# Two PSUM banks for products of weights and one for the transposes and rows behind them, in place of a shared set of three

## The chip, the cores and the metric

The kernel runs on one core of one Trainium2 chip. The metric is the device time of one execution in microseconds (us); lower is better. Time before is a median of three executions, and one further execution was profiled.

## The reference

One layer of a hybrid decoder, 2048 tokens behind 16 meta tokens, width 1024, everything in float32. The normalised input is projected by one wide matrix; the parts feed three causal mixers of four heads of 128 each (stick-breaking attention, a gated delta rule called GDN here, and HGRN2, called HG); each mixer's output is gated, projected by its own branch matrix, weighted by a sigmoid mix and summed; the sum is projected once more and added to the input.

```
xn = rms_norm(h, norm_w)
proj = einsum('btd,dn->btn', xn, w_in)          # 12*512 + 8 + 3*1024 columns
o_sb = stick_breaking_attention(rms_norm(q), rms_norm(k), v) * silu(sb_z)
o_gd = rms_norm(gated_delta_rule_chunked(l2_norm(gq), l2_norm(gk), gv, beta, g)) * silu(gd_z)
o_hg = rms_norm(hgrn2_chunked(silu(hg_q), hk, hg_i, log(forget))) * silu(hg_z)
gates = sigmoid(mix)                            # (b, t, 3, 1024)
y = sum over the three branches of gates[b] * einsum('btw,wd->btd', o_b, w_branch[b])
out = h + einsum('btd,de->bte', y, w_out)
```

## The kernel before, in words

The tokens are worked in four groups of 512 (`j` = 0 to 3; group 0 carries the 16 meta tokens too and computes them in two halves of 272 and 256 columns). Everything is held transposed: width on the 128 partitions, tokens in the free dimension. Every float32 product is three matmuls (`mm3`, lines 167 to 169): the operands are split in a high and a low part, and high by high, high by low and low by high are summed in one PSUM bank. A projection by 128 columns of a weight matrix is therefore 24 matmuls of 128x512 (8 pieces of the width, three each) into one bank.

The dense stream (`dense_work`) yields after each piece: per group, attention's projections (`sb_proj`, four heads), GDN's rows and projections (`gdn_rows`, `gdn_proj`, `gdn_gates`), HG's (`hg_proj`), the branch products (`branch`) and the output (`outp`). The three scans, attention (`z`, `tr` and `av` tiles, lines 521 to 565), GDN (855 to 1023) and HG (1151), are chains of small steps over TensorE (PE), ACT, DVE and POOL; `weave` advances the dense stream between their steps in proportion to estimated times, so that PE has products of weights to run while a chain is on another engine. The emitted program is reordered afterwards by the framework's scheduler, so a change of buffers changes the order on every engine. A product that stands between two steps of a scan is called a filler here.

The eight PSUM banks: four for `z` and `tr` (scan tiles), one for `av` (attention's output), three called `acc`. All of `acc` comes from one rotating function, `p_acc`, whether the tile is a projection of 24 matmuls or the four small transposes behind it. Such followers are: the column sums of squares (`sum_cols`, transposes at L380 in `to_tokens`), the broadcast of a row of scales back over the partitions (`row_bcast`, L176 and for the meta tokens L180), the turn of the values into token order (`post_v`, L380), GDN's rows (`gdn_rows`, L700) and HG's first state (L1117). Each is read by ACT, DVE or both (for example L454, which multiplies the keys by the row) and its bank is free again when the last reader is done. They are put off by `later` to the end of the next projection, so they come out between two projections. While the GDN and HG scans run (`n_acc[1]` true) every fourth tile of `p_acc` goes to the `av` bank, which attention doesn't use then.

Line numbers are those of the kernel before; in the kernel after the same lines stand 9 or 10 lower (L167 is L176, L176 is L185, L380 is L389, L558 is L567), and tile numbers are 3 higher.

Of the kernel before, what the change touches and what calls it, by code (L numbers as in the profile page):

```python
# [7 lines left out]
F32 = mybir.dt.float32  # L8
# [4 lines left out]
PSUM = bass.MemoryType.PSUM  # L13
DRAM = bass.MemoryType.DRAM

P = 128
# [23 lines left out]
def kernel(  # L40
# [21 lines left out]
    nc = tc.nc  # L62
# [3 lines left out]
    wpool = ctx.enter_context(tc.tile_pool(name="wpool", bufs=3))  # L66
    pool = ctx.enter_context(tc.tile_pool(name="pool", bufs=2))
    dram = ctx.enter_context(tc.tile_pool(name="dram", bufs=1, space=DRAM))
    ps_acc = ctx.enter_context(tc.tile_pool(name="ps_acc", bufs=3, space=PSUM))
    ps_z = ctx.enter_context(tc.tile_pool(name="ps_z", bufs=4, space=PSUM))  # L70
    ps_av = ctx.enter_context(tc.tile_pool(name="ps_av", bufs=1, space=PSUM))

# [2 lines left out]
    def nm(s):  # L75
        uid[0] += 1
        return f"{s}_{uid[0]}"
# [6 lines left out]
        return pool.tile(list(shape), dt, tag=tag, name=nm(tag), bufs=bufs or BUFS[tag])  # L84


    n_acc = [0, False]

    def p_acc():
        n_acc[0] += 1  # L90
        if n_acc[1] and n_acc[0] % 4 == 0:
            return ps_av.tile([P, 512], F32, tag="av", name=nm("av"))
        return ps_acc.tile([P, 512], F32, tag="acc", name=nm("acc"))

    def p_z():
        return ps_z.tile([P, 512], F32, tag="z", name=nm("z"))
# [74 lines left out]

    def row_bcast(r, cols, mcol):

        pt = p_acc()
        for n, c in enumerate(cols):
            nc.tensor.transpose(pt[:, n * P : (n + 1) * P], r[:, c : c + 1].broadcast_to([P, P]), ident)  # L176
        res = [(slice(META, WQ), pt)]
        if mcol is not None:
            pm = p_acc()
            nc.tensor.transpose(  # L180
                pm[:, :META], r[:META, mcol : mcol + 1].broadcast_to([META, P]), ident[:META, :META]
            )
            res.append((slice(0, META), pm[:, :META]))
        return res
# [10 lines left out]
    def norm_x0():  # L195

        xt, sq, raws = [], [], []
        for k in range(KC):
            t = slot("D")
# [7 lines left out]
        for k in range(KC):  # L207
            t = slot("D")
# [10 lines left out]
        ps = p_acc()  # L219
# [13 lines left out]
        xl = [xpool.tile([P, WQ], F32R, tag=f"xl{k}", name=nm("xl")) for k in range(KC)]  # L233
        rows = []
        for i, (a, b) in enumerate(HALVES):
            rb = p_acc()
            c = 0
            if i == 0:
                nc.tensor.transpose(
                    rb[:, :META], r[:META, NT : NT + 1].broadcast_to([META, P]), ident[:META, :META]  # L240
                )
                c = META
            for n in (2 * i, 2 * i + 1):
                nc.tensor.transpose(rb[:, c : c + P], r[:, n : n + 1].broadcast_to([P, P]), ident)
                c += P
            rows.append(rb)
# [115 lines left out]

    def sum_cols(src, dst, c, meta_c=None, ps=None):

        ps = ps or p_acc
        pt = to_tokens(src, ps())
        nc.vector.tensor_reduce(
            dst[:, c : c + NT], pt.rearrange("p (n d) -> p n d", n=NT), mybir.AxisListType.X, ALU.add
        )
        if meta_c is not None:  # L370
            pm = ps()
            nc.tensor.transpose(pm[:META, :P], src[:, :META], ident)
            nc.vector.tensor_reduce(
                dst[:META, meta_c : meta_c + 1], pm[:META, :P], mybir.AxisListType.X, ALU.add
            )
# [33 lines left out]
    def sb_proj(j, xs, h, st):  # L409
# [64 lines left out]
        vm = slot("vmp", (96, HD), F32R, 2) if m0 else None  # L474

        def post_v():
            pt = to_tokens(vraw, p_acc())
            nc.scalar.copy(vh, pt)
            sub_lo(vl, pt, vh, nc.vector)
            if m0:  # L480
                pm = p_acc()
                nc.tensor.transpose(pm[:META, :P], vraw[:, :META], ident)
                nc.scalar.copy(vm, zero1[:96].broadcast_to([96, HD]))
                for r0 in (0, 32):
                    nc.scalar.copy(vm[r0 : r0 + META], pm[:META, :P])
                sub_lo(vm[64 : 64 + META], pm[:META, :P], vm[:META], nc.vector)
            if j < nq - 1:
                dv = [dram.tile([P, TQ], F32, name=nm("dv")) for _ in range(2)]
                for s_, d_ in ((vh, dv[0]), (vl, dv[1])):
                    nc.sync.dma_start(d_, s_.bitcast(F32))  # L490
                dm = []
                if m0:
                    dm = [dram.tile([96, HD], F32, name=nm("dm"))]
                    nc.sync.dma_start(dm[0], vm.bitcast(F32))
                d_kv[(j, h, "v")] = dv + dm
# [142 lines left out]
    def gdn_rows(j, xs, st):  # L638
# [12 lines left out]
        bcol = slot("bcol", (P, H, 5), F32, 2)  # L651

        def post():
            pt = p_acc()
            for n in range(NT):
                nc.tensor.transpose(
                    pt[:, n * nr : n * nr + nr], raw[:nr, META + n * P : META + (n + 1) * P], ident[:nr, :nr]
# [1 line left out]
            c8 = slot("c8", (P, 2, H, 5), F32, 1)  # L659
            if m0:  # L660
                nc.gpsimd.memset(c8, 0.0)
                pm = p_acc()
                nc.tensor.transpose(pm[:META, :36], raw[:36, :META], ident[:36, :36])
                for q in range(2):
                    nc.vector.tensor_copy(c8[:META, q, :, 4], pm[:META, 32 * q : 32 * q + H])
# [30 lines left out]
            later(lambda: post_rows(ab))  # L696

        def post_rows(ab):
            pr = p_acc()
            nc.tensor.transpose(pr[:, :P], ab, ident)  # L700
            row = slot("D", (P, 2, P))
            nc.scalar.copy(row[:, 0], pr[:, :P])
            sets = [(0, 16, P, rows)] + ([(64, H, META, rowsm)] if m0 else [])
            for p0, np_, w, dst in sets:
                al_ = row[p0 : p0 + np_, 0, :w]
                eg = row[p0 : p0 + np_, 1, :w]
                nc.vector.tensor_tensor_scan(
                    eg, al_, zero1[p0 : p0 + np_].broadcast_to([np_, w]), 1.0, ALU.mult, ALU.add
                )
                nc.vector.memset(al_[:, 0:1], 0.0)  # L710
                be = row[p0 + 32 : p0 + 32 + np_, 0, :w]
                for i, src in enumerate((al_, eg, be)):
                    nc.sync.dma_start(dst[i].rearrange("h (n t) -> (h n) t", t=w), src)
# [29 lines left out]
    def gdn_proj(j, xs, hs, st):  # L743
# [5 lines left out]
        def head(h):  # L749
# [37 lines left out]
            bvm = slot("bvm", (META, P), F32, 4) if m0 else None  # L787

            def post_v():
                pt = to_tokens(vv, p_acc())  # L790
                for n in range(NT):
                    nc.scalar.mul(bv[:, n], pt[:, n * P : (n + 1) * P], bs[:, n : n + 1])
                if m0:
                    pm = p_acc()
                    nc.tensor.transpose(pm[:META, :P], vv[:, :META], ident)
                    nc.scalar.mul(bvm, pm[:META, :P], bcol[:META, h, NT : NT + 1])

# [274 lines left out]
    def hg_proj(j, xs, h, st):  # L1072
# [23 lines left out]
        yield from proj(j, xs, CH_HI + h, True, lambda ps, a, b: nc.scalar.copy(vraw[:, a:b], ps))  # L1096
        vt = slot("D", (P, NT, P))
        def post_v():
            nc.scalar.copy(vt.rearrange("p a b -> p (a b)"), to_tokens(vraw, p_acc()))
            if m0:  # L1100
                pm = p_acc()
                nc.tensor.transpose(pm[:META, :P], vraw[:, :META], ident)
                vm = slot("vm", (META, P), F32, 2)
                nc.scalar.copy(vm, pm[:META, :P])
# [4 lines left out]
                    1.0, ALU.mult, ALU.add,  # L1109
                )  # L1110
                nc.vector.tensor_mul(km, km, kk[:, :META])
                pm = p_acc()
                nc.tensor.transpose(pm[:META, :P], km, ident)
                kmt = slot("kmt", (META, P), F32, 2)
                nc.scalar.copy(kmt, pm[:META, :P])
                pm = p_acc()
                nc.tensor.matmul(pm[:, :P], kmt, vm, start=True, stop=True)  # L1117
                nc.scalar.copy(Sh[h], pm[:, :P])

# [227 lines left out]
    def dense_work():  # L1347

        xs = norm_x0()
        for j in range(nq):  # L1350
            y, yh, yl = [None] * KC, [None] * KC, [None] * KC
            pool_share[0] = 5
            for h in range(H):
                yield from sb_proj(j, xs, h, sst)
                if j == 0 and h == 0:
                    load_levels()
            ahead = 5 * (j >= AHEAD)
# [247 lines left out]
```

## Time and profile before

| | |
|---|---|
| median of three executions | 2745.89 us (2745.52 to 2747.46) |
| profiled execution | 2744.01 us, span 2742.2 us |
| mean granted TensorE clock | 0.996 of full speed |
| PE busy | 2693.8 us, 98% of the span |
| DVE, ACT, POOL busy | 1433.0, 961.7 and 724.1 us |

PE's busy time is counted by the rows of its matmuls, whose modelled ends overlap the next start; time in which it stood is 48 us in all, 11.8 of them in the first wait after the start.

### The profile page before, as it was taken

How to read it: one execution, taken by the hardware profiler on the slowest of the kernel's cores; microseconds unless marked ns; L12 is line 12 of the kernel's file. 1: busy time of each engine (PE TensorE's matmuls, PEld its weight loads, DVE VectorE, ACT ScalarE, POOL GpSimd, SP SyncE). 2: the span in 40 equal slices, each digit the busy share in tenths (PEclk: the TensorE clock that was granted, in tenths of full speed). 3: DMA queues.
4: the chain of work that ended last, by engine and by line, in shares of the span. 5: the costliest groups of instructions: out<-in, count | busy, mean ns of one | idle time of the engine just before them, and what ended most of it. 6: DMA issues, size and time to landing. Idle time of an engine off the chain costs nothing.

```text
span 2742.2 us, 46669 instructions
## 1 busy us (share of the span) xinstructions
PE 2693.8 (98%) x17984; PEld 2248.8 (82%) x17984; DVE 1433.0 (52%) x2870; ACT 961.7 (35%) x2199; POOL 724.1 (26%) x989
## 2 busy tenths in 40 slices
PE   7999999999999999999999999999999999999999
PEld 6898788888888888888888888878888887787887
DVE  5467638635357634443255765553325577456522
ACT  5554244343346212212144641221224455312120
POOL 4555203333132401112022340111212233302111
PEclk9999999999999999999999999999999999999999
DMA  7667756679554654557755556355764454554556
GB/s 263 228 209 245 256 184 222 229 266 321 195 183 142 209 177 129 156 162 243 226 185 168 164 177 186 109 156 155 252 214 146 159 166 138 159 157 124 163 164 212
DMA packets 200834, 521.08 MB, mean 190 GB/s; under 512 B 42848, under 2 KB 44832, under 8 KB 200612
## 3 DMA queue, kind: packets, MB, share of 16 engines
q1 hardware_dynamic: 200324, 518.03, 58.7%
q8 instruction: 142, 2.33, 0.3%
q14 instruction: 80, 0.66, 0.1%
q10 hardware_dynamic: 288, 0.07, 0.0%
HBM read 397.57 MB, written 120.44 MB: 189 GB/s over the span
## 4 chain that ended last, share of the span: by engine, by line
PE 92%; DVE 4%; ACT 1%; DMA 1%; issue 1%; POOL 1%; SPq 0%; DVEq 0%; POOLq 0%; ACTq 0%
PE acc L167 21%; PE acc L168 21%; PE acc L169 21%; PE av L167 4%; PE av L168 4%; PE av L169 4%; PE tr L558 2%; PE acc L380 2%; PE z L167 1%; PE z L1151 1%; PE z L169 1%; PE z L168 1%; PE z L855 1%; PE tr L380 1%; PE tr L1236 1%
## 5 line engine op out<-in xcount | busy, mean ns | idle before, releaser
L167 PE MATMUL acc<-xh,w 128*128 128x512 f32 (+2 forms) x2248 | 858.4, 382 | 4.1 <-DVE D L454 2.2
L168 PE MATMUL acc<-xl,w 128*128 128x512 f32 (+2 forms) x2248 | 847.3, 377 | 0.3 <-DVE xl L260 0.2
L169 PE MATMUL acc<-xh,w 128*128 128x512 f32 (+2 forms) x2248 | 845.4, 376 | 1.7 <-DVE w L118 1.7
L167 PEld LDWEIGHTS acc<-xh,w 128*128 128x128 f32 x2248 | 426.4, 190 | 78.9 <-DVE D L454 3.0
L169 PEld LDWEIGHTS acc<-xh,w 128*128 128x128 f32 x2248 | 426.4, 190 | 74.6 <-DVE w L118 2.2
L168 PEld LDWEIGHTS acc<-xl,w 128*128 128x128 f32 x2248 | 426.1, 190 | 69.8 <-DVE xl L260 1.3
L530 DVE TENSOR_TENSOR_SCAN S<-S,zero 128x128 f32<-128x128 f32 (+4 forms) x216 | 199.8, 927 | 151.3 <-ACT S L524 124.0
L118 POOL TENSOR_TENSOR w<-wraw,w 128x512 fp32r<-128x512 f32 x106 | 147.9, 1396 | 274.5 <-ACT w L147 228.1
L536 POOL TENSOR_TENSOR S<-S,S 128x256 f32<-128x256 f32 (+2 forms) x108 | 96.2, 891 | 372.0 <-DVE S L530 232.2
L524 ACT ACTIVATE S<-z,rq 128x128 f32<-128x128 f32 (+4 forms) x216 | 117.0, 542 | 140.4 <-PE z L169 94.4
L147 ACT CAST w<-wraw 128x512 fp32r<-128x512 f32 x182 | 112.4, 619 | 132.9 <-PE acc L169 68.8
L736 DVE SCALAR_TENSOR_TENSOR D<-D,cw,D 128x512 f32<-128x512 f32 (+1 forms) x144 | 120.8, 839 | 21.9 <-ACT D L734 19.4
L118 DVE TENSOR_TENSOR S<-tr,S 128x512 fp32r<-128x512 f32 (+4 forms) x176 | 105.9, 607 | 44.9 <-ACT S L563 25.8
L167 PE MATMUL acc<-ob,w 128*128 128x512 f32 x312 | 124.6, 401 | 1.4 <-ACT ob L401 1.4
L168 PE MATMUL acc<-ob,w 128*128 128x512 f32 x312 | 124.5, 399 | 0.0
L169 PE MATMUL acc<-ob,w 128*128 128x512 f32 x312 | 123.7, 396 | 0.6 <-issue 0.6
L1288 POOL TENSOR_TENSOR y<-y,g 128x512 f32<-128x512 f32 x32 | 51.7, 1616 | 263.6 <-DVE g L1286 263.6
L167 PE MATMUL av<-xh,w 128*128 128x512 f32 (+2 forms) x304 | 118.5, 390 | 0.7 <-ACT D L1082 0.7
L168 PE MATMUL av<-xl,w 128*128 128x512 f32 (+2 forms) x304 | 117.7, 387 | 0.0
L169 PE MATMUL av<-xh,w 128*128 128x512 f32 (+2 forms) x304 | 117.0, 385 | 0.0
L525 ACT ACTIVATE S<-z,rq 128x128 f32<-128x128 f32 (+4 forms) x216 | 116.5, 539 | 0.0
L558 PE MATMUL tr<-ident,S 128*128 128x128 f32 (+1 forms) x608 | 102.0, 272 | 2.0 <-POOL S L536 1.7
(391 smaller groups left out, 4781.5 us busy)
## 6 DMA issues: line engine op xcount, KB each, us to landing
w<-wk SPq DMA_DIRECT2D x555, 512.0 KB, 3.6
wk<-w SPq DMA_DIRECT2D x184, 512.0 KB, 3.5
wraw<-in_w_in_dram SPq DMA_DIRECT2D x142, 256.0 KB, 4.1
D<-in_xq_dram SPq DMA_DIRECT2D x56, 256.0 KB, 4.5
S<-rows SPq DMA_DIRECT2D x48, 256.0 KB, 5.0
S<-dv SPq DMA_DIRECT2D x48, 256.0 KB, 4.6
out_dram<-D SPq DMA_DIRECT2D x32, 256.0 KB, 4.8
S<-dk SPq DMA_DIRECT2D x24, 264.0 KB, 4.1
```

The costliest lines, as they stand in the source:

```text
L118: (eng or nc.gpsimd).tensor_sub(out_, a, hi.bitcast(F32))
L147: nc.scalar.copy(hi, raw)
L167: nc.tensor.matmul(dst, lh, rh, start=first, stop=False)
L168: nc.tensor.matmul(dst, lh, rl, start=False, stop=False)
L169: nc.tensor.matmul(dst, ll, rh, start=False, stop=last)
L380: nc.tensor.transpose(pt[:, n * P : (n + 1) * P], src[:, META + n * P : META + (n + 1) * P], ident)
L524: nc.scalar.activation(pc[:, :n], z[:, :n], AF.Sigmoid, scale=rq[:, NT + i : NT + i + 1])
L525: nc.scalar.activation(at[:, :n], z[:, :n], AF.Sigmoid, scale=rq[:, i : i + 1])
L530: nc.vector.tensor_tensor_scan(pc[:, 0:n][:, ::-1], pc[:, 0:n][:, ::-1], zero1.broadcast_to([P, n]), 1.0 if carry[i] is None else pc[:, n ...
L536: eng.tensor_mul(at[:, :n], at[:, :n], pc[:, 1 : n + 1])
L558: nc.tensor.transpose(tr[:kw, i * P : (i + 1) * P], ats[i][:, a - lo : a - lo + kw], ident)
L736: nc.vector.scalar_tensor_tensor(dst[:, c0:], raw[:, c0 + i : c0 + i + n], cw[:, ci, i : i + 1], dst[:, c0:], ALU.mult, ALU.add)
```

## The change

`ps_acc` shrinks from three banks to two, and a new pool `ps_t` of one bank takes the followers: `p_t` replaces `p_acc` in `row_bcast`, `sum_cols`, the rows of the first norm, all three `post_v` and GDN's rows. Until a flag `n_acc[2]` is set, behind the first head's attention projections of group 0, `p_acc` and `p_t` together rotate through the same three banks as before. From then on products alternate between two banks, and while the GDN and HG scans run every third product, not every fourth, goes to the `av` bank. The number of banks (eight), the instructions and their counts are the same on every engine; the tiles are 378 `acc`, 181 `t` and 93 `av`, against 571 `acc` and 81 `av`.

```diff
-    ps_acc = ctx.enter_context(tc.tile_pool(name="ps_acc", bufs=3, space=PSUM))
+    ps_acc = ctx.enter_context(tc.tile_pool(name="ps_acc", bufs=2, space=PSUM))
+    ps_t = ctx.enter_context(tc.tile_pool(name="ps_t", bufs=1, space=PSUM))
...
-    n_acc = [0, False]
+    n_acc = [0, False, False]
     def p_acc():
         n_acc[0] += 1
-        if n_acc[1] and n_acc[0] % 4 == 0:
+        if not n_acc[2] and n_acc[0] % 3 == 0:
+            return ps_t.tile([P, 512], F32, tag="t", name=nm("t"))
+        if n_acc[1] and n_acc[0] % 3 == 0:
             return ps_av.tile([P, 512], F32, tag="av", name=nm("av"))
         return ps_acc.tile([P, 512], F32, tag="acc", name=nm("acc"))
+
+    def p_t():
+        if not n_acc[2]:
+            return p_acc()
+        return ps_t.tile([P, 512], F32, tag="t", name=nm("t"))
...
     def row_bcast(r, cols, mcol):
-        pt = p_acc()
+        pt = p_t()
...
     def sum_cols(src, dst, c, meta_c=None, ps=None):
-        ps = ps or p_acc
+        ps = ps or p_t
...
         def post_v():
-            pt = to_tokens(vraw, p_acc())
+            pt = to_tokens(vraw, p_t())
...
                 yield from sb_proj(j, xs, h, sst)
+                n_acc[2] = True
```

The change moves instructions. The first place is on PE in group 1's attention projections, where a row of scales for the keys (`acc_8163`, later `t_8166`) and a set of column sums (`acc_8175`) stood between two products. Before:

```order
3679 L176 MATMUL acc_8163<-ident,nr_8123 128x128 [waits Activation_49,Pool_49]
3680 L176 MATMUL acc_8163<-ident,nr_8123 128x128 x3
3681 L380 MATMUL acc_8175<-ident,D_8086 128x128 [waits DVE_49]
3682 L380 MATMUL acc_8175<-ident,D_8086 128x128 x3
3683 L167 MATMUL acc_8193<-xh_7639,w_1570_8189 128x512 [waits DMAHW6_49,DVE_49]
3684 L168 MATMUL acc_8193<-xl_7640,w_1570_8189 128x512
```

The same place on PE after, where the product is called `acc_8196`:

```order
3686 L176 MATMUL acc_8196<-xh_7738,w_1570_8192 128x512
3687 L177 MATMUL acc_8196<-xl_7739,w_1570_8192 128x512
3688 L185 MATMUL t_8166<-ident,nr_8126 128x128 [waits DVE_49,Pool_49]
3689 L185 MATMUL t_8166<-ident,nr_8126 128x128 x3
3690 L178 MATMUL acc_8196<-xh_7738,w_1570_8192 128x512
3691 L176 MATMUL acc_8196<-xh_7786,w_1570_8192 128x512
```

The row now comes after the eighth matmul of the product, in the bank of its own, and the column sums (`t_8178`) come another 16 matmuls of this product and seven of the next later.

The second place is on PE in group 0's projections for GDN (`gdn_proj`), where a head's row of scales for 512 tokens and for the 16 meta tokens (`nr_2745`) is broadcast and its values (`D_2537`) are turned. Before, all of it stands between two products:

```order
1327 L169 MATMUL acc_2802<-xh_172,w_554_2769 128x256
1328 L176 MATMUL acc_2829<-ident,nr_2745 128x128 [waits DVE_49,Pool_49]
1329 L176 MATMUL acc_2829<-ident,nr_2745 128x128 x3
1330 L180 MATMUL acc_2834<-ident,nr_2745 128x16 [waits Activation_49]
1331 L380 MATMUL acc_2838<-ident,D_2537 128x128 [waits Activation_49]
1332 L380 MATMUL acc_2838<-ident,D_2537 128x128 x3
1333 L795 MATMUL acc_2847<-ident,D_2537 16x128 [waits DVE_49]
1334 L167 MATMUL acc_2887<-xh_165,w_570_2873 128x272 [waits DVE_49]
```

On PE after, the row for the 512 tokens stands inside the next product, 18 matmuls ahead of these rows, which begin with the last matmul of that product:

```order
1371 L178 MATMUL acc_2916<-xh_175,w_573_2883 128x256
1372 L189 MATMUL t_2837<-ident,nr_2748 128x16 [waits DVE_49]
1373 L389 MATMUL t_2841<-ident,D_2540 128x128 [waits DVE_49]
1374 L389 MATMUL t_2841<-ident,D_2540 128x128 x3
1375 L864 MATMUL z_2937<-S_2868,D_2280 128x128 [waits DVE_49]
1376 L864 MATMUL z_2937<-S_2868,D_2280 128x128 x3
```

The wait for ACT ahead of the values is gone; the meta row, the values and GDN's first z tile now each wait for DVE.

The third place is on PE at the end of an attention head in group 3. `z` tiles take queries and keys, `tr` tiles turn attention weights, `av_22290` collects the output. Before:

```order
10950 L521 MATMUL z_22911<-neg_b,ident_b 128x128
10951 L558 MATMUL tr_22857<-ident,S_22848 32x128 [waits Pool_49]
10952 L558 MATMUL tr_22869<-ident,S_22848 128x128
10953 L558 MATMUL tr_22879<-ident,S_22848 128x128
10954 L167 MATMUL z_22932<-D_22420,D_22303 128x256 [waits DVE_49]
10955 L168 MATMUL z_22932<-D_22421,D_22303 128x256
10956 L169 MATMUL z_22932<-D_22420,D_22304 128x256
10957 L521 LDWEIGHTS ident_b
10958 L521 MATMUL z_22932<-neg_b,ident_b 128x128
10959 L547 MATMUL av_22290<-S_22862,vmp_22645 128x512 [waits Activation_49]
10960 L167 MATMUL av_22290<-S_22874,S_22639 128x512
```

On PE after, the turned weights are followed by products of weights, and the output's first matmul (L556, for `av_22293`) comes behind them:

```order
10938 L567 MATMUL tr_22860<-ident,S_22851 32x128 [waits Pool_49]
10939 L567 MATMUL tr_22872<-ident,S_22851 128x128
10940 L567 MATMUL tr_22882<-ident,S_22808 128x128
10941 L567 MATMUL tr_22882<-ident,S_22834 128x128
10942 L567 MATMUL tr_22882<-ident,S_22851 128x128
10943 L176 MATMUL acc_23936<-xh_20810,w_4659_23934 128x512
10944 L177 MATMUL acc_23936<-xl_20811,w_4659_23934 128x512
10945 L178 MATMUL acc_23936<-xh_20810,w_4659_23934 128x512
10946 L176 MATMUL acc_24001<-xh_20544,w_4671_23997 128x512 [waits DMAHW0_49,Activation_49]
10947 L177 MATMUL acc_24001<-xl_20545,w_4671_23997 128x512
```

Between the last `tr` row and the output's first matmul now stand 25 matmuls of two products and four transposes of a follower; before there were none. At the end of the next head (`av_22910`) it is the other way: `acc_24403` and `acc_24453`, of which 24 and nine matmuls stood inside the head's last blocks, come behind its last output matmul.

## Rows read from the trace of the kernel before

**Rows 1.** The page's part 1: busy time, share of the span, instructions.

```profile
PE 2693.8 (98%) x17984; PEld 2248.8 (82%) x17984; DVE 1433.0 (52%) x2870; ACT 961.7 (35%) x2199; POOL 724.1 (26%) x989
```

**Rows 2.** PE's waits: us in total, times, longest.

```profile
PE acc L221 <- DVE D L212: 11.8, 1, 11.8
PE z L1151 <- DVE S L1142: 4.8, 4, 2.4
PE acc L380 <- ACT D L731: 3.3, 3, 2.2
PE acc L700 <- DVE D L694: 2.6, 1, 2.6
PE acc L167 <- DVE D L454: 2.2, 4, 1.0
PE acc L239 <- POOL nr L231: 2.0, 1, 2.0
PE av L547 <- ACT S L565: 2.0, 1, 2.0
PE z L167 <- DVE S L118: 1.9, 1, 1.9
PE acc L169 <- DVE w L118: 1.7, 1, 1.7
PE tr L558 <- POOL S L536: 1.7, 1, 1.7
...
PE z L943 <- DVE S L927: 1.1, 1, 1.1
...
PE acc L380 <- ACT D L1096: 0.7, 1, 0.7
PE av L167 <- ACT D L1082: 0.7, 1, 0.7
```

**Rows 3.** Timeline around 707 us: start, length, instruction, idle before it.

```profile
707.44 0.60 PE L380 MATMUL acc<-ident,D 128*128 128x128 f32 x4
707.64 0.75 DVE L454 SCALAR_TENSOR_TENSOR D<-D,wk,acc 128x512 f32<-128x512 f32 x1 [2.96 <-PE acc L176]
...
708.44 0.51 PE L167 MATMUL acc<-xh,w 128*128 128x512 f32 x1 [0.40 <-DVE D L454]
...
709.25 0.39 PE L167 MATMUL acc<-xh,w 128*128 128x512 f32 x1
...
709.48 0.39 PE L168 MATMUL acc<-xl,w 128*128 128x512 f32 x1
```

**Rows 4.** Stretches: length, busy time per engine, then PEclk, DMA share, GB/s.

```profile
212.00:224.00 12.00, 8.87 (x52) 8.32 (x51) 8.34 (x12) 5.11 (x13) 5.91 (x5) 0.72 0.70 229
1788.00:1798.00 10.00, 7.65 (x119) 6.02 (x118) 10.00 (x25) 3.25 (x9) 1.28 (x1) 0.83 0.40 126
2270.00:2286.00 16.00, 12.10 (x59) 9.41 (x58) 11.75 (x17) 9.81 (x21) 2.37 (x10) 0.79 0.31 100
2343.00:2370.00 27.00, 22.54 (x122) 18.33 (x121) 13.47 (x22) 8.90 (x20) 6.88 (x14) 1.00 0.37 105
2496.00:2514.00 18.00, 15.89 (x463) 12.69 (x463) 18.00 (x51) 1.63 (x5) 5.27 (x2) 1.00 0.43 122
```

**Rows 5.** Timeline around 214 us, group 0's GDN projections.

```profile
211.80 2.29 POOL L125 TENSOR_TENSOR nr<-nu,mhalf 128x9 f32<-128x9 f32 x1
...
214.15 0.65 PE L176 MATMUL acc<-ident,nr 128*128 128x128 f32 x4 [0.93 <-POOL nr L125]
...
216.74 0.35 ACT L731 COPY D<-acc 128x256 f32<-128x256 f32 x1
...
217.15 1.11 PE L380 MATMUL acc<-ident,D 128*128 128x128 f32 x4 [2.20 <-ACT D L731]
```

**Rows 6.** PE's timeline at 2281 us, the output matmuls of an attention head.

```profile
2281.25 0.63 PE L168 MATMUL av<-S,S 128*128 128x512 f32 x1
2281.68 0.63 PE L169 MATMUL av<-S,S 128*128 128x512 f32 x1
```

More of the change, by code (lines that the diff above doesn't have):

```diff
@@ L178, in row_bcast @@
         if mcol is not None:
-            pm = p_acc()
+            pm = p_t()
             nc.tensor.transpose(
@@ L235, in norm_x0 @@
         for i, (a, b) in enumerate(HALVES):
-            rb = p_acc()
+            rb = p_t()
             c = 0
@@ L480, in post_v @@
             if m0:
-                pm = p_acc()
+                pm = p_t()
                 nc.tensor.transpose(pm[:META, :P], vraw[:, :META], ident)
@@ L653, in post @@
         def post():
-            pt = p_acc()
+            pt = p_t()
             for n in range(NT):
@@ L661, in post @@
                 nc.gpsimd.memset(c8, 0.0)
-                pm = p_acc()
+                pm = p_t()
                 nc.tensor.transpose(pm[:META, :36], raw[:36, :META], ident[:36, :36])
@@ L698, in post_rows @@
         def post_rows(ab):
-            pr = p_acc()
+            pr = p_t()
             nc.tensor.transpose(pr[:, :P], ab, ident)
@@ L789, in post_v @@
             def post_v():
-                pt = to_tokens(vv, p_acc())
+                pt = to_tokens(vv, p_t())
                 for n in range(NT):
@@ L793, in post_v @@
                 if m0:
-                    pm = p_acc()
+                    pm = p_t()
                     nc.tensor.transpose(pm[:META, :P], vv[:, :META], ident)
@@ L1098, in post_v @@
         def post_v():
-            nc.scalar.copy(vt.rearrange("p a b -> p (a b)"), to_tokens(vraw, p_acc()))
+            nc.scalar.copy(vt.rearrange("p a b -> p (a b)"), to_tokens(vraw, p_t()))
             if m0:
-                pm = p_acc()
+                pm = p_t()
                 nc.tensor.transpose(pm[:META, :P], vraw[:, :META], ident)
@@ L1111, in post_v @@
                 nc.vector.tensor_mul(km, km, kk[:, :META])
-                pm = p_acc()
+                pm = p_t()
                 nc.tensor.transpose(pm[:META, :P], km, ident)
@@ L1115, in post_v @@
                 nc.scalar.copy(kmt, pm[:META, :P])
-                pm = p_acc()
+                pm = p_t()
                 nc.tensor.matmul(pm[:, :P], kmt, vm, start=True, stop=True)
```

## The prediction

> **What bounds the kernel now.** I read the page first, then PE's waits over the whole span, then the busy time and granted clock of the stretches in which those waits lie, and last the timelines there. The page shows a kernel that is bound by PE: it is busy for 2693.8 us, DVE for about half the span, ACT and POOL for less [rows 1]. The reader is to see in the list of waits how little there is to win [rows 2]: PE stands for 2742.2 - 2693.8 = 48 us, and 13.8 of them belong to the first norm (L221 and L239), which the change leaves in the old rotation; what remains is at most 35 us, in many places. The stretches [rows 4] show a second cost: three of them have a mean granted clock of 0.72 to 0.83. PE was idle for 2 to 4 us in each, and part of each ran at 1.2 GHz. The output matmuls at 2281 us start 0.43 us apart [rows 6], against 0.23 at full clock [rows 3]. So a wait in these places costs more than its own length, and the change can win a wait of 2 us twice.
>
> Not all waits are for a bank. L1151 waits for DVE's chain of HG, L558 and the z product at L167 for attention's chain, L700 and L176 for rows. A new rotation reaches those only by the order of instructions.
>
> **The change part by part.** The instructions are the same, so PE's busy time stays, and each term is a wait gained or lost. A wait costs a little more than the list shows, because a matmul's row of 0.39 us overlaps the next start, 0.23 behind it [rows 3]: 0.16 us for each.
>
> *A, the joins of attention's projections.* At 707 us the row's reader, L454, takes DVE 0.75 us, the column sums on PE cover only part of it, and the next product takes over the row's bank and waits 0.40 [rows 3]. There are four such waits, 2.2 us in sum [rows 2], in groups 1, 2 and 3; with the overlap 2.2 + 4 x 0.16 = 2.8. After, the next product takes a bank of its own and the row comes eight matmuls into it; its reader has 16 + 7 matmuls (5.3 us) to be done before the bank t is wanted again. I take all: -2.8 (bounds -2.2 and -2.8).
>
> *B, two more waits for a bank.* The product that follows the values of HG in `av` (0.7) and the values behind L1096 (0.7) [rows 2]. By the order after, no turn of the `av` bank has under 3 us of PE work between, where one had 0.13; the other keeps a part. -1.2 (bounds -0.7 and -1.7).
>
> *C, group 0's GDN projections.* At 214 us POOL's power takes 2.29 us, the row waits 0.93 for it, and then the values wait 2.20 for L731, which frees a bank late because it stands in ACT's queue behind work that waits for DVE [rows 5]. PE is idle 12.00 - 8.87 = 3.1 us in this stretch, and its clock of 0.72 means 2 x 0.28 x 12 = 6.7 us at 1.2 GHz [rows 4]; the values' wait lies in these, so at least 6.7 - 2.2 = 4.5 us were worked at half rate, which loses 2.2. Another 3.3 - 2.2 = 1.1 us of waits for L731 stand elsewhere [rows 2]. Together 6.4. After, the row lies inside a product, but the meta row, the values and the first z tile follow each other with no product between, two of them in one bank. Each waits for a DVE reading; the nearest row is L454's 0.75 [rows 3], with the way there and back about 1 us each, so 2 us for the two heads in which this order appears. -4.5 (bounds -6.4, and 0 if two short waits set off the same clock).
>
> *D, GDN's scan, first step.* L943 waits 1.1 for DVE [rows 2]; it stands some 13 us of PE work later after. -1.2 with the overlap. The wait of 1.7 for a weight's low part, 3 us on, is left, as nothing there changes the load.
>
> *E, HG's scans in groups 2 and 3.* L1151's four waits, 4.8 us [rows 2]. DVE is busy 10.00 of 10 and 18.00 of 18 us there [rows 4], so the chain itself does not shorten; only products put between its steps help. In group 3 the steps now stand 1.6 to 6.4 us of PE work apart, where they came in pairs: -1.5 of the 2.1 idle. In group 2 the order is nearly the same: -0.5. Bounds 0 and -6 (all waits, and 3.4 us of half clock from 0.83 of 10 us).
>
> *F, the end of an attention head in group 3.* From 2270 to 2286 PE is idle 3.9 us, and 0.79 means 6.7 us at half clock [rows 4]. At most 1.9 of these were the second wait, so 4.8 at half rate lose 2.4: 6.3 in all. After, 25 matmuls and four transposes (25 x 0.23 + 4 x 0.11 = 6.2 us) stand between the turned weights and the output. They cover the waits of 1.7 and 1.9 [rows 2]. I leave 1.3 for the z product's half of the chain: -5.0 (bounds -6.3 and -3).
>
> *G, what F and the new order take from elsewhere.* Fillers are not made, only moved. Counting PE work between products of weights in the two orders (a z product of 272 columns as 0.13, a transpose as 0.11): the next head loses 24 + 9 matmuls from its last blocks, and a stretch of 9.0 us without a filler appears there (2.8 and 2.5 before); a further one of 8.2 us appears some 15 us before F; GDN's scan has one of 10.1 in group 0 that is new, and 14.4 in place of 10.2 in group 2. The trace of before prices such a stretch: 6.3 in F, where it is 7.9 us long. But L547's and the branch product's waits at the end of the next head already cost 4.5 us idle at full clock in 2343 to 2370 [rows 4], and stay. I take about half of F's price for the first (+3.0), a quarter for the second, whose chain starts with work in hand (+1.5), and +0.8 for GDN's, which has four heads' chains in hand at once. +5.3 (bounds 0 and +14).
>
> What comes out even: L700 (2.6 [rows 2]), the same chain at the same distance; `post_v` and `sum_cols` where a product of 24 matmuls already lay on both sides; the changed order on DVE, ACT, POOL and SP, which have idle time in nearly all stretches.
>
> Sum: -2.8 - 1.2 - 4.5 - 1.2 - 2.0 - 5.0 + 5.3 = -11.4. The profiled execution took 2744.0, which gives 2732.6; the median lies 1.9 above the profiled one, so 2734.5.
>
> **A rule against the change.** The new bank t does not rotate: two followers in succession meet the same bank. In the order after, of the bank's 180 turns six have under 1 us of PE work between the last write of one tile and the first of the next, and 19 under 2.5; of the 568 turns in the old set of three 22 were under 1 us. The Trainium skill (Perfetto Trace Analysis, Optimizing Tensor Performance, Matmuls) says that independent groups should rotate through different PSUM banks, so that reading one out overlaps the next. The trace agrees where the turn is short (0.40 at 707 us), and by the rule alone the 19 turns lose; by distance only the six do, and two of those are in C.
>
> **The rivals.** First, *no measurable change*: each of the 19 short turns of bank t waits for its reader, on average 0.5 us (between 0.40 and 0.75, [rows 3]): +9.5, and the sum is -1.9, 2744. For it: followers come in pairs in group 0. Against it: most of the 19 have over 2 us between, more than a reader of 0.75 needs.
>
> Second, *slower*: attention in group 3 runs out of fillers. Its price is F's 6.3 for each stretch, at the ends of heads. Without G the gains are 16.7; from three and a half such stretches on (22) the kernel is slower by over 5.5. If all four heads' ends in group 3 did so: -16.7 + 25.2 = +8.5, 2754. For it: fillers left the second head, and half clock follows such waits [rows 4]. Against it: I count only two new stretches of that length in attention.
>
> Third, *a larger gain*: ACT, DVE and POOL have run ahead when the filler-free stretches come, and G is nothing: -16.7, 2729.
>
> **How the numbers follow.** The forecast has 0.46, no change 0.24, slower 0.12, the larger gain 0.18. 0.2% of the time is 5.5 us, about what this measurement can tell from no change; the forecast and the larger gain lie beyond it: faster 0.64, same 0.24, slower 0.12. The forecast is 2734.5. The range goes down to 2724 (the larger gain, with C and E at their bounds) and up to 2750 (no change, and a part of the slower case); its own range is 2729 to 2740.
>
> **What would show it.** In the profile after: no wait of a product for L454; at 2270 to 2286 less than 2 us idle and a clock near 1; around 214 us waits under 1.3 us for DVE and no wait for L731; at the end of the next attention head in group 3 longer waits than 2.0 and 1.4. The prediction is wrong if a clock under 0.9 appears in new stretches of attention or of GDN's scan, if followers wait for their own bank in many places, or if HG's waits decide.

## The result and the profile after

The changed kernel took 2729.69 us (median of six; 2728.32 to 2733.25) against 2746.68 for the kernel before measured beside it: a ratio of 0.9943 with a 95% interval of 0.9932 to 0.9953, 15.7 us faster than before. The forecast was 2734.5. The profiled execution's span fell from 2742.2 to 2728.1 us, by 14.1 where my sum says 11.4.

The page's part 1 of the kernel after, beside [rows 1]:

```profile
PE 2690.0 (99%) x17984; PEld 2243.4 (82%) x17984; DVE 1432.5 (53%) x2870; ACT 961.0 (35%) x2199; POOL 717.7 (26%) x989
```

PE stands for 2728.1 - 2690.0 = 38.1 us, 10.3 less than before. The other 3.8 us of the gain are busy time. Work at half clock (TensorE's lower level, 1.2 in place of 2.4 GHz) that is gone is part of it: the mean granted clock rose from 0.996 to 0.999. How large a part isn't shown.

PE's waits after, beside [rows 2] (us in total, times, longest):

```profile
PE acc L230 <- DVE D L221: 11.9, 1, 11.9
PE z L1160 <- DVE S L1151: 2.3, 2, 1.4
PE acc L248 <- POOL nr L240: 2.0, 1, 2.0
PE av L556 <- ACT S L574: 2.0, 1, 2.0
PE acc L176 <- DVE y L1293: 1.7, 1, 1.7
PE acc L176 <- ACT ob L410: 1.4, 1, 1.4
PE z L973 <- DVE S L958: 1.4, 1, 1.4
PE z L864 <- DVE S L843: 1.2, 2, 0.6
PE acc L176 <- ACT D L1091: 1.1, 2, 0.6
...
PE t L189 <- DVE D L782: 0.8, 1, 0.8
PE t L389 <- ACT D L767: 0.7, 1, 0.7
...
PE t L389 <- DVE D L782: 0.5, 2, 0.3
PE acc L176 <- DVE D L127: 0.5, 1, 0.5
PE t L185 <- POOL nr L134: 0.5, 1, 0.5
```

No product waits for L463 (L454 before) any more; of the single waits over 2 us after the start (L700, L731, one of L1151) none is left. The followers' own bank costs little: the `t` rows shown sum to 2.5 us, and of these only the 1.3 us for L782, which reads an earlier tile of `t`, can be waits for the bank. L767 and L134 write what the transposes read.

Stretches of the kernel after that answer to [rows 4] (length, busy time per engine, PEclk, DMA share, GB/s), and, first, the one around L709 (L700 before):

```profile
158.00:174.00 16.00, 15.97 (x132) 15.55 (x131) 9.60 (x23) 13.14 (x30) 7.83 (x13) 1.00 0.60 200
208.00:224.00 16.00, 15.03 (x122) 14.04 (x122) 12.99 (x18) 8.55 (x22) 11.83 (x16) 1.00 0.77 275
1770.00:1790.00 20.00, 18.61 (x353) 14.51 (x352) 20.00 (x52) 2.27 (x8) 3.15 (x2) 1.00 0.45 136
2248.00:2258.00 10.00, 8.62 (x52) 6.84 (x51) 9.18 (x16) 6.94 (x16) 2.75 (x6) 1.00 0.15 53
2258.00:2272.00 14.00, 14.00 (x74) 11.66 (x73) 11.48 (x20) 7.77 (x16) 4.60 (x12) 1.00 0.31 95
2328.00:2358.00 30.00, 23.93 (x138) 19.16 (x136) 17.40 (x24) 11.16 (x27) 11.37 (x22) 1.00 0.46 129
```

The end of the attention head at 2258 to 2272 has no idle time and full clock, where before it had 3.9 idle and 0.79. The price of it stands 10 us earlier (1.4 idle) and at the end of the next head (6.1 idle of 30, where 4.5 of 27 had been).

The timeline after at a join of group 1, beside [rows 3]:

```profile
703.83 0.60 PE L185 MATMUL t<-ident,nr 128*128 128x128 f32 x4
704.18 0.48 PE L178 MATMUL acc<-xh,w 128*128 128x512 f32 x1
704.46 0.75 DVE L463 SCALAR_TENSOR_TENSOR D<-D,wk,t 128x512 f32<-128x512 f32 x1 [0.91 <-PE t L185]
704.50 0.39 PE L176 MATMUL acc<-xh,w 128*128 128x512 f32 x1
```

The reader's 0.75 us lie beside the product's matmuls, which start as if nothing stood between them.

**Where the time came from.** To compare runs whose orders differ, I priced every matmul by the usual distance to the next start for its kind and neighbours, the same price in all kernels, and compared the times of two runs at equal summed price. The difference, split at the same points of work, in us against before (negative is faster; stretches by their time in the kernel before; "forecast" by my terms):

| stretch of before | what lies there | forecast | after | phase 1 | phase 2 | every 4th | every 2nd | shared in scans | own in scans only | shared, every 3rd |
|---|---|---|---|---|---|---|---|---|---|---|
| 87 to 173 | GDN's rows | 0 | -3.1 | -3.1 | -3.1 | -3.1 | -3.3 | -3.1 | -1.8 | 0.2 |
| 173 to 281 | GDN's projections, group 0 (C) | -4.5 | -0.2 | 0.3 | 2.0 | 1.7 | 0.0 | 0.0 | 2.5 | 0.2 |
| 281 to 407 | GDN's scan, group 0 (D, part of G) | -0.8 | -0.2 | -0.6 | -0.1 | -0.7 | 3.4 | -2.5 | 3.1 | 2.9 |
| 407 to 1691 | a join each in groups 1 and 2, one av wait (A, B) | -1.8 | -2.1 | -2.0 | -2.2 | 5.4 | 0.6 | -1.1 | -0.8 | 6.5 |
| 1760 to 1816 | HG, group 2 (E) | -0.5 | -3.7 | -3.6 | 0.0 | -0.2 | -2.3 | -1.7 | 0.2 | -5.4 |
| 1816 to 2245 | two joins (A) | -1.7 | -2.3 | -2.4 | -2.6 | -2.4 | 0.3 | -2.5 | 0.9 | 1.1 |
| 2245 to 2298 | end of a head, group 3 (F, part of G) | -3.5 | -5.0 | -5.0 | -5.0 | -5.0 | -5.0 | -4.6 | -2.7 | 0.7 |
| 2298 to 2395 | end of the next head (G) | 3.0 | 2.4 | 4.5 | 2.4 | 2.4 | 4.7 | 3.5 | 1.6 | 0.5 |
| 2479 to 2544 | HG, group 3 (E) | -1.5 | -1.1 | -1.1 | 2.8 | 2.8 | -0.7 | 2.4 | 2.7 | -3.0 |
| whole | | -11.4 | -14.1 | -12.5 | -5.0 | 2.4 | 2.4 | -9.3 | 6.0 | 10.7 |

The columns are the experiments below (phase 1 and phase 2 are the remainders of 1 and 2 in the last of them); differences under 1 us between two profiles carry little. C's row depends on the pricing: with prices by the next neighbour alone its -0.2 for the kernel after becomes about -1.7, while no other row of that column moves by more than 0.3. And one stretch can differ by the clock alone: the kernel with the bank t from the first instruction (below) has the same order as after at the end of the next head, but its profiled execution worked part of it at half clock, and that of after, shown above, did not:

```profile
2328.00:2358.00 30.00, 25.04 (x124) 19.83 (x123) 16.59 (x25) 10.28 (x24) 10.19 (x18) 0.89 0.35 100
```

At equal work this is worth 1.4 us.

One thing has to be known for reading the columns. `n_acc[0]`, whose remainder decides which product goes to `av`, counts every tile that `p_acc` hands out. Where an experiment gives followers back to `p_acc`, it also shifts which products go to `av` afterwards.

### The profile page after: what moved, and what is told of

It reads as the page before. It is cut to its first block, busy times and chain, and to the rows that moved or that the text cites. A ratio compares the mean times of both kernels' runs of the same rounds, so it can differ in the third digit from the quotient of the medians.

```text
span 2728.1 us, 46691 instructions
## 1 busy us (share of the span) xinstructions
PE 2690.0 (99%) x17984; PEld 2243.4 (82%) x17984; DVE 1432.5 (53%) x2870; ACT 961.0 (35%) x2199; POOL 717.7 (26%) x989
## 4 chain that ended last, share of the span: by engine, by line
PE 92%; DVE 5%; DMA 1%; ACT 1%; issue 1%; POOL 0%; SPq 0%; DVEq 0%; ACTq 0%; POOLq 0%
PE acc L176 20%; PE acc L177 20%; PE acc L178 20%; PE av L176 5%; PE av L177 5%; PE av L178 5%; PE tr L567 2%; PE t L389 2%; PE z L1160 1%; PE z L176 1%; PE z L177 1%; PE z L178 1%; PE z L864 1%; PE tr L389 1%; PE tr L1245 1%
## 5 line engine op out<-in xcount | busy, mean ns | idle before, releaser
L176 PE MATMUL acc<-xh,w 128*128 128x512 f32 (+2 forms) x2096 | 796.8, 380 | 5.6 <-DVE y L1293 1.7
L177 PE MATMUL acc<-xl,w 128*128 128x512 f32 (+2 forms) x2096 | 790.0, 377 | 0.3 <-DVE xl L269 0.2
L178 PE MATMUL acc<-xh,w 128*128 128x512 f32 (+2 forms) x2096 | 786.7, 375 | 0.0
L176 PEld LDWEIGHTS acc<-xh,w 128*128 128x128 f32 x2096 | 396.1, 189 | 75.2 <-DVE y L1293 2.2
L178 PEld LDWEIGHTS acc<-xh,w 128*128 128x128 f32 x2096 | 396.4, 189 | 66.2 <-issue 0.2
L177 PEld LDWEIGHTS acc<-xl,w 128*128 128x128 f32 x2096 | 395.9, 189 | 65.2 <-DVE xl L269 1.3
L176 PE MATMUL av<-xh,w 128*128 128x512 f32 (+2 forms) x440 | 172.7, 392 | 0.0
L177 PE MATMUL av<-xl,w 128*128 128x512 f32 (+2 forms) x440 | 171.9, 391 | 0.0
L178 PE MATMUL av<-xh,w 128*128 128x512 f32 (+2 forms) x440 | 171.3, 389 | 0.0
L176 PE MATMUL acc<-ob,w 128*128 128x512 f32 x296 | 118.0, 399 | 1.4 <-ACT ob L410 1.4
L177 PE MATMUL acc<-ob,w 128*128 128x512 f32 x296 | 117.7, 398 | 0.0
L178 PE MATMUL acc<-ob,w 128*128 128x512 f32 x296 | 117.6, 397 | 0.0
L133 POOL TENSOR_SCALAR nu<-nv 128x8 f32<-128x8 f32 (+3 forms) x39 | 14.8, 379 | 334.2 <-DVE nv L1065 193.6
```

What stands on the lines that cost most here:

```text
L176: nc.tensor.matmul(dst, lh, rh, start=first, stop=False)
L177: nc.tensor.matmul(dst, lh, rl, start=False, stop=False)
L178: nc.tensor.matmul(dst, ll, rh, start=False, stop=last)
```

## The experiments

Two theories. By the first, the banks give the time: followers with slow readers no longer hold banks that products want. By the second, the time comes from the order that the framework's reordering makes of the new banks, and a small change of the rule would give another. All ratios are to the kernel before, measured beside them.

**Every fourth product to av.**

```diff
-        if n_acc[1] and n_acc[0] % 3 == 0:
+        if n_acc[1] and n_acc[0] % 4 == 0:
```

> The kernel after, but every fourth product instead of every third goes to the av bank while the scans run. If the gain comes from the bank of its own for the followers, nearly all of it stays: 13 to 17 us faster than before. If the larger share of the av bank gives the scans' part of it (the profile after has 4 us less lost in HG's scan of group 2 and 1 us less at the join behind L1082), that part goes: 9 to 12 us faster than before.

Measured 2744.15 us, 0.9994 (0.9986 to 1.0003): the whole gain is gone, which neither case held. Waits that are new or longer than in the kernel after:

```profile
PE z L1160 <- DVE S L1151: 5.3, 4, 2.2
PE acc L176 <- DVE g L1295: 2.9, 1, 2.9
...
PE acc L176 <- ACT D L1279: 2.0, 1, 2.0
```

HG's scans have half clock again (0.89 and 0.88):

```profile
1782.00:1798.00 16.00, 13.84 (x266) 10.89 (x265) 16.00 (x40) 3.63 (x10) 3.46 (x2) 0.89 0.43 134
2497.00:2511.00 14.00, 11.60 (x349) 9.20 (x348) 14.00 (x37) 0.60 (x1) 2.47 (x2) 0.88 0.34 107
```

L1295 multiplies a branch product out of its bank, on a DVE that is in a scan; L1279 is a gate's sigmoid on ACT. With two banks and every fourth product elsewhere a product meets them and waits; the wait for L1295 stands in HG's scan of group 0 and costs 4.5 of the 7.5 us that this kernel loses against after in the table's row from 407 to 1691. Outside the scans the table shows this kernel as good as after (-3.1, -2.4, -5.0).

**Shared set of three, every third to av.**

```diff
-        if n_acc[1] and n_acc[0] % 4 == 0:
+        if n_acc[1] and n_acc[0] % 3 == 0:
```

> The kernel before with its shared set of three banks, but every third tile to the av bank while the scans run. If the followers' own bank is the cause, this gives little: within 4 us of before, and the waits for L454 in attention's projections (2.2 us in four) stay. If the av share is the cause in the scans, 4 to 6 us faster, all of it in GDN's and HG's scans.

Measured 2753.6 us, 1.0026 (1.0015 to 1.0036): slower, outside both expectations. L454's waits are as before (2.2 in four). HG's scans gain 5.4 and 3.0, but two other stretches, worked partly at half clock, cost 12 (the first lies in HG's second scan of group 0):

```profile
530.00:542.00 12.00, 11.74 (x51) 9.32 (x52) 7.20 (x22) 1.99 (x4) 2.59 (x2) 0.76 0.28 91
2445.00:2465.00 20.00, 17.62 (x276) 15.12 (x277) 9.67 (x30) 5.22 (x18) 2.80 (x10) 0.83 0.34 91
```

**The bank t for rows alone.** `row_bcast` keeps `p_t`; all other calls become `p_acc`.

```diff
     def sum_cols(src, dst, c, meta_c=None, ps=None):
-        ps = ps or p_t
+        ps = ps or p_acc
...
-            pt = to_tokens(vraw, p_t())
+            pt = to_tokens(vraw, p_acc())
```

> The kernel after, but only row_bcast (the rows that a DVE multiplication of 0.75 us reads) has the bank t; column sums, values and GDN's rows rotate with the products over two banks. If the gain needs a bank free of all followers, the four joins and group 0's projections lose again: 0 to 8 us faster than before, with new waits of products for ACT's and DVE's copies. If the rows alone were the trouble, 12 us or more faster.

Measured 2787.55 us, 1.0156 (1.0142 to 1.0170): far slower. Products now wait for the readers of column sums (L376, L382) and of GDN's values (L801), and, with two banks for all, longer for readers of products (L740, L398):

```profile
PE acc L176 <- DVE nv L376: 5.9, 8, 1.5
PE acc L176 <- ACT D L801: 3.6, 4, 1.1
PE acc L176 <- ACT D L740: 3.2, 6, 0.9
PE acc L176 <- DVE nv L382: 3.1, 3, 1.1
PE acc L176 <- DVE D L398: 3.0, 4, 1.2
```

So two banks are too few for products and these followers together. Column sums, values and GDN's rows went back at once, and the count for `av` shifted with them; which of them has to stay out isn't shown by this run.

**GDN's rows back in the products' banks.** `post` and `post_rows` of `gdn_rows` use `p_acc`.

```diff
         def post_rows(ab):
-            pr = p_t()
+            pr = p_acc()
```

> The kernel after, but GDN's rows (post and post_rows in gdn_rows) take their banks from the products' two again. The wait of 2.6 us for L694 at 165 us, which I had expected to stay and which is gone in the profile after, comes back if it was a matter of the bank: 2 to 4 us slower than after. If the wait went because of the order around it alone, the time stays within 1.5 us of after.

Measured 2748.99 us, 1.0009 (1.0000 to 1.0018): 18 us slower than after by the ratios, all of the gain, though it touches two small followers per group (three in group 0). The wait of 2.6 us does not come back in group 0, but shorter ones before L709 do, one in group 0 and one in group 1:

```profile
PE acc L709 <- DVE D L703: 1.0, 1, 1.0
PE acc L709 <- DVE D L698: 0.8, 1, 0.8
```

In group 1 that wait and another of 0.9 come with half clock; first this kernel, then about the same place in the kernel after:

```profile
826.00:846.00 20.00, 18.25 (x87) 14.69 (x86) 12.34 (x29) 12.23 (x27) 1.36 (x9) 0.91 0.41 122
823.00:843.00 20.00, 20.00 (x105) 16.21 (x104) 14.05 (x31) 14.07 (x30) 1.48 (x10) 1.00 0.50 145
```

Priced as for the table, this place costs 3.8 us against after, and another 2.6 are lost around GDN's rows of group 3. So the edited places do take part of the loss. HG's scan of group 2 takes another 3.8, and there the count is the reason: seven tiles more are counted by then, and this kernel's order on PE is that of the kernel with a remainder of 2 (last experiment), which loses the same there. The largest part lies at the end of attention's next head (2298 to 2395), 10.3 us against before, where the kernel after loses 2.4:

```profile
2326.00:2376.00 50.00, 43.84 (x226) 35.04 (x225) 32.25 (x55) 22.11 (x48) 17.34 (x28) 0.93 0.35 105
```

Nothing was edited in that stretch and its order differs from that of after; that the reordering of what stands ahead of it is the cause is argued, not shown.

**Old rule inside the scans, new rule outside.**

```diff
     def p_acc():
         n_acc[0] += 1
+        if n_acc[1] and n_acc[0] % 4 == 0:
+            return ps_av.tile([P, 512], F32, tag="av", name=nm("av"))
-        if not n_acc[2] and n_acc[0] % 3 == 0:
+        if (n_acc[1] or not n_acc[2]) and n_acc[0] % 3 == 0:
             return ps_t.tile([P, 512], F32, tag="t", name=nm("t"))
-        if n_acc[1] and n_acc[0] % 3 == 0:
-            return ps_av.tile([P, 512], F32, tag="av", name=nm("av"))
         return ps_acc.tile([P, 512], F32, tag="acc", name=nm("acc"))
...
     def p_t():
-        if not n_acc[2]:
+        if n_acc[1] or not n_acc[2]:
             return p_acc()
```

> The kernel after outside the GDN and HG scans (two banks for products, t for followers); inside them the old rule: one set of three for all, every fourth to av. If the followers' bank gives the attention's part and the av share the scans' part, and the two add, this keeps the joins of attention (3 us) and the end of the head in group 3 (5 us): 7 to 11 us faster than before, with the waits for L1151's counterpart near 4.8 us again. If the two only work together, within 4 us of before.

Measured 2735.21 us, 0.9970 (0.9959 to 0.9981): 8.2 us faster, as expected if the parts add. L1160's waits sum to 7.1 us in five, and HG's scan of group 3 has half clock:

```profile
2495.00:2515.00 20.00, 16.96 (x280) 13.48 (x280) 20.00 (x50) 4.32 (x11) 3.36 (x2) 0.91 0.42 134
```

**New rule inside the scans only.** The mirror image: the first clause of `p_acc` and the test of `p_t` hold wherever the scans do not run, and every third product goes to av inside.

```diff
-        if not n_acc[2] and n_acc[0] % 3 == 0:
+        if not (n_acc[1] and n_acc[2]) and n_acc[0] % 3 == 0:
             return ps_t.tile([P, 512], F32, tag="t", name=nm("t"))
...
-        if not n_acc[2]:
+        if not (n_acc[1] and n_acc[2]):
             return p_acc()
```

> The other half: the old shared set of three outside the scans, and inside them the new rule (two banks and every third product in av, followers in t). If the parts add: 4 to 7 us faster than before, all of it in the scans; the four waits for L454 stay (2.2 us) and so does the half clock at the end of the head in group 3. If they only work together, within 3 us of before.

Measured 2752.28 us, 1.0030 (1.0019 to 1.0042): slower, which neither case held. By the times the parts do not add: outside gives -8, inside alone +8, and both -16. But the scans here are not those of after. Followers outside the scans are counted again, so other products go to `av`, and HG's scans stand on PE in the order of the kernel with a remainder of 2, which alone loses 8 us of the gain: without the 8 us that the rule outside gives, that kernel would be 1 us slower than before. This run is 8 slower, so some 7 us remain, and whether the parts add with the same scans is open. Its named signs failed too: the wait for L463 (L454 before) is there once and not four times, and the end of the head in group 3 has full clock and half of the gain (-2.7). Outside the scans tiles take turns in three banks as before, and there followers wait for L740 (L731 before) and products for L398 as before or more:

```profile
PE acc L389 <- ACT D L740: 2.7, 2, 1.9
...
PE t L389 <- ACT D L740: 2.2, 1, 2.2
...
PE acc L176 <- DVE D L398: 1.8, 3, 0.6
```

**Every second product to av.** The clause with `% 2`.

> The kernel after, but every second product goes to av while the scans run. From every fourth to every third the time fell by 16 us. If what counts is how long each of the products' banks rests, av in turn with two banks is evenest at every third, and this is 3 to 10 us slower than after, with new waits of av products for their own bank's readers. If the two banks are what holds the products, it is 2 to 6 us faster than after.

Measured 2744.31 us, 1.0000 (0.9991 to 1.0009): 16 us slower than after by the ratios, beyond the 3 to 10 of the first case. The longest new wait is GDN's, 3.0 us for L936 in group 0's scan, with a clock of 0.72 from 335 to 347 us. The av products do wait for their own bank's readers, 4.3 us:

```profile
PE av L176 <- ACT D L1279: 1.8, 1, 1.8
...
PE av L176 <- DVE y L1293: 1.4, 2, 1.2
PE av L176 <- DVE g L1295: 1.1, 1, 1.1
```

**The bank t from the first instruction.** `n_acc = [0, False, True]`.

> The kernel after without the first flag: the followers' bank from the first instruction, products in two banks. Only the first head of group 0 differs by intent. If the first norm's rows and products need three banks in turn, 2 to 6 us slower than after, all of it before 100 us. If the rest of the order changes with it and decides, the loss or gain lies behind 100 us.

Measured 2733.25 us, 0.9962 (0.9949 to 0.9974), 5 us slower than after by the ratios, though the two intervals touch. At equal work its profile lies 2.9 us behind that of after once the first norm and its first products are done, before 62 us, as the first case has it. The rest of the difference is the half clock at the end of the next head, in the same order as after (see the row under the table). In those first products two wait 2.1 us for L426, which squares a product in its bank; in after it is 0.5:

```profile
PE acc L176 <- ACT D L426: 2.1, 2, 1.5
```

**The reordering off, before and after.**

```diff
-    with tile.TileContext(nc, schedule_with_timeline_sim=True) as tc:
+    with tile.TileContext(nc, schedule_with_timeline_sim=False) as tc:
```

> The kernel before with the framework's reordering off, so that each engine runs its instructions nearly in the order in which they are written. Read only against the next run. Its own time against before says what the reordering is worth: 1 to 10% slower than before by either theory.

> The kernel after with the reordering off. On PE 14983 of 15213 instructions then stand as in the run above, and the banks are what differs. If the banks themselves give the time (no product waits for a follower's reader), this is 5 to 20 us faster than the run above, and waits of products for L454 and its like are gone. If the time comes from the order that the reordering makes of the new banks, it is within 4 us of the run above, or slower by the followers' turns in their one bank.

Measured 2836.02 us (1.0335; 1.0320 to 1.0349) and 2831.10 us (1.0312; 1.0297 to 1.0328). 4.9 us lie between the medians, between the two cases, and with four executions each the intervals overlap, so that even the sign of the banks' own effect is not settled here; it isn't the 16 us. The waits say why. Before, in this order:

```profile
PE acc L380 <- ACT D L752: 7.9, 3, 3.5
PE acc L380 <- ACT D L731: 7.3, 3, 4.0
...
PE acc L167 <- DVE D L454: 2.1, 6, 0.4
```

After, in nearly the same order:

```profile
PE t L389 <- ACT D L801: 12.7, 4, 4.7
...
PE t L189 <- DVE D L782: 5.1, 2, 2.6
```

Products no longer wait for L454, and the waits for L731 (9.8 us in all, 2.5 of them of a product) are gone. But followers wait for the earlier follower in their one bank. The 5.1 us for L782 are such waits. The 12.7 for L801 are so only in part: L752 (L761 after) writes the squares that these transposes read, and L801, which reads the bank, comes next on ACT. At 949 us before, PE waits 2.74 for the squares; at 954 us after, at the same place, 3.94 until L801 is done. So the bank moves waits from products to followers. That it becomes time only with the reordering, which puts products ahead of a waiting follower (as in the orders shown at the beginning), is argued from these waits.

**The same share of av, one place on, and two.** The clause with `% 3 == 1`, and with `% 3 == 2`.

> The kernel after, where the products that go to av while the scans run are those with a remainder of 1, not 0, of their number by three: as many of them, one place on. If the share of av is what counts, within 3 us of after. If it matters which products stand where in the order, 4 to 17 us slower, since the kernel with every fourth and that with every second both lost all of the gain.

> The same with a remainder of 2. As for remainder 1: within 3 us of after if the share counts, 4 to 17 us slower if the place counts. The two together say how far one time of such an order can be read as the effect of its rule.

Measured 2728.53 us, 0.9946 (0.9934 to 0.9959), and 2737.13 us, 0.9973 (0.9963 to 0.9983). The first is the same as after. The second loses about 8 us by the ratios, most of it in HG's scans: 3.0 us idle of 20 in group 2, 2.9 and a clock of 0.91 in group 3, with L1160's waits at 5.8 us in five:

```profile
1774.00:1794.00 20.00, 17.00 (x301) 13.64 (x301) 18.59 (x46) 5.05 (x13) 5.85 (x2) 1.00 0.43 134
2484.00:2504.00 20.00, 17.10 (x370) 13.69 (x371) 20.00 (x45) 3.00 (x5) 7.34 (x5) 0.91 0.28 86
```

So even at the same share the place of the products decides half of the gain. The kernel before was not run with other remainders of four, so how far its own time is that of one order is open.

## Why the prediction was right, and where it was not

- **A, the joins: right.** All four waits of products for the row's reader are gone. The stretch with two joins alone measures -2.3 (-1.7 forecast), the one with two joins and B's `av` wait -2.1 (-1.8 forecast).
- **B: right for one, not for the other.** The wait for L1096 (L1105 after) is gone; waits of products for L1082 (L1091 after) remain, 1.1 us in two, in an `acc` bank and not in `av`.
- **C, GDN's projections: mis-sized.** I had -4.5; measured -0.2 over the stretch. The wait for L731 is gone and the clock stays at 1.00, as I said. What failed is the count of what comes instead: I priced two short waits at 2 us, and the list after has six there (L864 and L389 two each, L189, L185), 3.0 us. The -0.2 itself is uncertain by some 2 us, since it depends on the pricing (above); PE's idle time in the stretch fell from 4.3 us in 108.0 to 3.1 in 106.3. The time shows less than the 4.5 either way, and where the rest went is open.
- **"L700, the same chain at the same distance": wrong.** The wait of 2.6 us and its half clock went, -3.1. PE is busy for 15.97 of 16 us there: L709 stands behind products of weights that cover the chain on ACT and DVE. I had compared its distance from its own predecessor and not what stands between. Where these rows use the products' banks again, L709 waits 1.0 and the half clock is gone as well: 15.03 us busy of the same 16 at 1.00, against 13.43 at 0.89 before. So most of it was the order, and the rest may be their bank.
- **E: mis-sized in group 2, right in group 3.** I had -0.5 and -1.5; measured -3.7 and -1.1. The prediction read the order of group 2 as nearly the same, and it isn't: before, 192, 128 and 96 of L1151's matmuls stood in a row with no product of weights between them; after, the rows of them are 128, three times 64, and 96. One wait of 1.4 in place of two that sum to 3.0 also saves the half clock of 0.83. That it hangs on places is shown by the phases: in phase 1 the counts and the gain are those of after, in phase 2 the 192 and 128 are back and the gain is nothing.
- **F and its counterpart: right, and larger.** -3.5 forecast with the stretch before it, -5.0 measured. All kernels of the table with a third pool have it, 2.7 us at least, and the shared set doesn't. The 2.7 are those of the kernel whose rule outside the scans is the old one, so about half of it needs no bank of their own for attention's followers.
- **G: right in size at the next head** (+3.0 and +2.4), but not in what it is made of. I expected longer waits than 2.0 and 1.4 there; the waits for L574 and L410 are 2.0 and 1.4 as before (L565 and L401 there). What is new is a wait of 0.8 (L567) and 1.7 in place of 1.0 for L1293 (L1284 before). GDN's scan in group 0 took back what its first step gained: L973 waits 1.4 and the clock from 342 to 354 us is 0.86. I had named a clock under 0.9 in GDN's scan as a sign of being wrong. It came, but the stretch is still 0.2 faster than before.

The total was right partly by luck, because two errors cancel: C gave 4.3 less by the table, GDN's rows and HG in group 2 gave 6.3 more. The rivals: bank t's turns (no change) did not decide in the order as it is. The Trainium skill (Perfetto Trace Analysis, Optimizing Tensor Performance, Matmuls) says that independent groups should rotate through different PSUM banks. The traces agree that a bank without rotation makes its next tile wait: 5.1 us for L782 with the reordering off, 1.3 in the kernel after, too little there to decide. Fillers running out (slower) fits the 10.3 us of one stretch in the kernel with GDN's rows moved back, and did not decide here either. The larger gain's time (2729) came out, but not its reason, that G is nothing. In its price of the slower case, three and a half times 6.3 less 16.7 is 5.35 and not over 5.5, which changes nothing else.

What is shown: column sums, values and GDN's rows in the products' two banks together cost 1.6% against before; GDN's rows alone cost the whole gain, part of it at their own places; the new rule outside the scans with the old one inside gives 8 us; and in the scans the place of the products in `av`, at the same share, is worth 8 us. That the share itself counts is less sure, since every fourth and every second also change the place. What is argued only: that the whole 16 us belong to this rule rather than to one good order. The three phases of the same rule give 0.9943, 0.9946 and 0.9973, all faster than before; with the reordering off the same banks differ by 4.9 us, which four executions each can't tell from nothing.

## What to carry to other kernels

When a reordering scheduler decides the order, a change of buffers is a change of order: read the order after, count the products that stand between a chain's steps, and price the wait that they cover with its half clock. Where small tiles with slow readers hold the banks of large products, a bank of their own can pay; here each group of them that was put back among two product banks cost the gain or more, and the products needed a third bank in turn where their own readers were slow. A counter that deals out banks ties places together: taking one tile out of the count shifts every later turn, so compare orders before calling two scans the same. Try neighbours of a rule that change nothing in kind (another remainder) before crediting the rule with all of a gain.

## What the runs showed that I had not expected

Two small tiles per group (three in group 0), put back in the products' banks, moved 8 us in a stretch of group 3 that holds none of them. Two kernels with the same order at the end of a head were profiled there once at full clock and once partly at half clock. And turning the reordering off costs 3.3%, six times what the banks gave with it.
